# Sparse attention: the compressed branch and the maxima as two streams of their own, with a new order in the scan, the last branch and the combinations

## Chip, core and metric

One Trainium2 chip, one of its cores. The metric is the time of one execution on the device in microseconds (us), as the median of several runs; lower is better. Engines are named as in the profile: PE (TensorE, matrix products; PEld is its weight load), DVE (VectorE), ACT (ScalarE), POOL (GpSimd), SP (SyncE, which issues nearly all DMAs).

## What is computed

A decoder block on 1024 positions of 1024 channels, all in float32. One input projection feeds three mixers; their outputs are projected, weighted with sigmoid gates, summed and projected once more; a gated MLP with a short convolution follows. What the change touches is this:

```python
# sparse attention, 2 key groups of 4 heads, per query t:
o_cmp = softmax(q @ kc + bias) @ vc              # over 63 compressed keys
idx   = top_8(block sums of that softmax)        # which 64-key blocks are selected
o_sel = softmax(q @ k_sel, keys of idx) @ v_sel
o_win = softmax(q @ k_win, last 512 keys) @ v_win
y_nsa = gate[0] * o_cmp + gate[1] * o_sel + gate[2] * o_win
# Mamba-2 scan, in chunks of 128: y = (C B^T * decay * dt) x + C state; then gating and a norm
mixed = g0 * (y_ssm @ w_br_ssm) + g1 * (y_sb @ w_br_sb) + g2 * (y_nsa @ w_br_nsa)
x = x + rms_norm(mixed @ w_out)
u = causal_conv(rms_norm(x) @ w_up)              # then gelu(gate) * val, @ w_down, norm, add
```

## The kernel before

Every float32 product of large matrices is made of three passes over rounded parts (hi times hi, hi times lo, lo times hi); a 128x1024 weight tile is loaded, ACT rounds it to `whi`, POOL subtracts to `wlo` (`load_w`, L290 to 300). All matrix instructions have source line L226, so they are told apart by the names of their tiles. A planner orders the instructions of each engine by its own timing model when the program is built; `tc.keep_in_program_order` pins PE to the order of the text while `in_order[0]` is set (in sparse attention and in the scan), and `tc.issue_after(x)` puts what a block emits on x's engine behind x in that engine's queue.

**Sparse attention** (`nsa_stage`) works on 16 query blocks: 2 groups `g` by 8 blocks of 128 queries `i`. For each, `compressed(g, i)` (L880 to 961) is a generator of nine steps: transposes and the 63 compressed scores, a softmax on DVE and ACT (L902 to L909), for i >= 4 the choice of key blocks down to `aug` (L917 to L930), three steps of nothing, transposes of the probabilities (`pT`, L937), one step later their product with `VC`, then the transposed queries `Q1`, `Q2`. `maxima(g, i)` (L963 to L1000) makes the row maxima of all scores, a product and a DVE reduction (L985) at a time: 8 of them for i < 4 and 16 above, then after `MM_LAG` = 3 steps four transposes and a copy into `Q1` (L1000). `attend()` is a generator that is sent one key block at a time: score, exp, rounding, and four slots later the product with the values; at the end of a branch `merge` and, at the end of a query block, `finish`. All these small pieces share single PSUM banks: `ps_b` has one buffer, `ps_o` one, `ps_s` and `ps_t` two.

The loop over n (L1083 to 1115) runs query block n in slots, the compressed branch of block n+2 and the maxima of block n+1 beside it. A slot sends one key block or none, takes one step of the compressed branch, one of the maxima, some fill (a step of fill is three 512-wide products of a gate projection: 176 steps in all), and one more step of the maxima:

```python
slots = max(NSA_SLOTS, len(blocks)) if n < 16 else NSA_LAG + 6
...
idle = next(ga, 0) == 0                 # compressed
if ready: idle = next(gb, 0) == 0 and idle      # maxima
fill.take(NSA_FILL[0] if b is None else NSA_FILL[1] + idle)
next(att)
if ready: next(gb, 0)
```

The number of key blocks is 2, 4, 6, 8, 10, 11, 12, 13 for i = 0 to 7, so there are 192 slots; 32 steps of fill come before the first.

**The scan** (`ssd_stage`) runs four generators `scan(q, ...)` in staggered turns: `front(c)` of chunk c makes decays `dec` (four ACT instructions L1324, an exp L1327), `ce`, `Bc` (L1343, L1344), `xd` (L1345) and their product (L1347); `back(c)` multiplies them on PE into `ps_b` or `ps_o`. Products of the other two branches (`branches`, L1472 on) fill between; at its end stand the first four half units (j = 0 to 3, first half of the positions) of the last branch, y_ssm @ w_br_ssm, two of them in `ps_s` and two in `dense` banks. `tail_stage` loads their gate rows (`ge`, L1586), multiplies (L1593), adds on POOL (L1594), and goes on with the remaining twelve half units in new `dense` banks.

**The MLP** starts with N_FIRST = 4 pairs of channel tiles made plainly (`up_half`, eight calls, each two units of 24 products, with the convolution L333 to L339 and at the end `gated`, L1728). All later pairs use a seven-product scheme; its right-hand sides are 16 sums and differences of the input (`combos`, L572 to L578, on DVE), rounded by ACT (L1859) and DVE (L1860, L1866).

Of the kernel before, what the change touches and what calls it, by code (L numbers as in the profile page):

```python
# [10 lines left out]
F32 = mybir.dt.float32  # L11
R32 = mybir.dt.float32r
# [205 lines left out]
def trunk(ctx: ExitStack, tc: tile.TileContext, A: dict, outT: bass.AP, dbg=None):  # L218
# [488 lines left out]

    part, ys, begun, weights = {}, {}, {}, {}
    ssd = ExitStack()
# [11 lines left out]
def nsa_stage(nc, tc, es, env):  # L721
# [160 lines left out]
    def compressed(g, i):  # L882
# [32 lines left out]
        if i >= 4:  # L915
# [26 lines left out]
        y = wk.tile([128, 4, 64], F32, name="yacc", bufs=4)  # L942
# [4 lines left out]
        Q1 = wk.tile([128, 512], R32, name="Q1", bufs=3)  # L947
        Q2 = wk.tile([128, 512], R32, name="Q2", bufs=3)
        p1 = ps_b()
# [131 lines left out]
    att = attend()  # L1081
    next(att)
    for n in range(-2, 17):  # L1083
        ga = compressed(*order[n + 2]) if 0 <= n + 2 < 16 else iter(())
        gb = maxima(*order[n + 1]) if 0 <= n + 1 < 16 else iter(())
# [7 lines left out]
        lead = min(NSA_LEAD, slots - nb)  # L1093
        cnt = slots - lead
        blocks = [None] * lead + [next(it) if (m + 1) * nb // cnt > m * nb // cnt else None for m in range(cnt)]
        if n == 7:
            next_keys(1, 0, 384)
            blocks += [None] * NSA_SWITCH[1]
        for m, b in enumerate(blocks):
            att.send(b)  # L1100
# [5 lines left out]
            idle = next(ga, 0) == 0  # L1106
            ready = n != 7 or m >= NSA_SWITCH[0]
            if ready:
                idle = next(gb, 0) == 0 and idle
            fill.take(NSA_FILL[0] if b is None else NSA_FILL[1] + idle)  # L1110
            next(att)
            if ready:
# [181 lines left out]
def ssd_stage(nc, tc, es, env):  # L1294
# [15 lines left out]
    def scan(q, x0, x1, B, C):  # L1310
# [7 lines left out]
        def front(c):  # L1318
# [22 lines left out]
            if c == 0:  # L1341
                states.append(wk.tile([128, 4, 64], F32, name="state"))
            V.tensor_tensor(Bc[:, 1], pt[:, 384:512], E.tri_i, op=OP.mult)  # L1343
# [128 lines left out]
    def branches(ys):  # L1472
        pairs = [(br, j0) for br in (2, 1) for j0 in range(0, 8, 2)]
        parts = [(0, 0), (1, 0), (0, 1), (1, 1)] + [(n, h) for n in range(2, 8) for h in range(2)]
        order = [(pairs[n][0], pairs[n][1] + m, h) for n, h in parts for m in range(2)]
        es = []

# [10 lines left out]
        for n, h in parts:  # L1488
# [15 lines left out]
            if n == 3:  # L1504
                ys[1, h] = sb_rows(h)
        gens = []
        for j in range(2):
            w = ws[8] if j == 0 else E.load_w(A["wb_ssm"][j], 1024)
            out = []
            gens.append(E.half_unit(Bank(), w, lambda k, h: E.ys[k, h], 8, 0, out))  # L1510
            yield from itertools.islice(gens[j], 6)
            E.begun[j, 0] = out[0]
        for g in gens:
            yield from g
        for j in range(2, 4):
            w = E.load_w(A["wb_ssm"][j], 1024)
            out = []
            yield from E.half_unit(E.psd, w, lambda k, h: E.ys[k, h], 8, 0, out)
            E.begun[j, 0] = out[0]
            E.weights[j] = w  # L1520

    held = E.ssm
# [12 lines left out]
    while n == 0 or any(gens):  # L1535
        if n in SSD_ROWS:
            with tc.issue_after(loaded[-1].ins):
                for q, ns, h in SSD_ROWS[n]:
                    E.ssm_rows(q, ns, E.third_t if q % 2 and ns[0] < 4 else E.row_t, h)
        for q, at in enumerate(SSD_AT):  # L1540
            if n == at:
                if q > 1:
                    acs[q] = ac_t(q)
                gens[q] = scan(q, *[held[q][m] for m in range(4)])
            if gens[q]:
                for m in range(1 + (n > at)):
                    if next(gens[q], 0) == 0:
# [14 lines left out]
def tail_stage(nc, tc, es, env):  # L1562
# [21 lines left out]
    for j, h in order:  # L1584
        e = bt.tile([128, 512], F32, name="ge")
        nc.sync.dma_start(e, E.g_d[j * 128:(j + 1) * 128, hs(h)])  # L1586
# [6 lines left out]
        V.tensor_tensor(e, ps, e, op=OP.mult)  # L1593
        P.tensor_tensor(e, E.part[h, j], e, op=OP.add)  # L1594
# [121 lines left out]
    halos = psn.tile([128, 512], F32, name="psn", tag="psn")  # L1716
    even = {}

# [363 lines left out]
```

## Time and profile before

| what | value |
|---|---|
| runs | 2216.98, 2216.97, 2218.39 us; median 2216.98 us |
| profiled execution | 2219.73 us, of which 2218.0 us lie between its first and last instruction |
| busy in the span | PE 2146.9 us (97%), DVE 1351.7 (61%), ACT 1216.8 (55%), POOL 1250.5 (56%) |
| chain that ended last | PE 83%, DVE 6%, ACT 3%, issue 3%, DMA 2%, POOL 2% |
| granted clock, mean | 0.991 |

A busy PE is not a PE at its peak: the ends of its instructions are modelled, so the rate is read from the number of products in a stretch. The waits view lists, for each engine, the time it sat idle and the instruction that ended that. [...]

### The profile page before, as it was taken

To read this page: it belongs to the slowest core of one execution; us is meant where nothing else is said; L and a number is where in the kernel's file an instruction comes from. 1 tells how busy PE (TensorE), PEld (TensorE's weight loads), DVE (VectorE), ACT (ScalarE), POOL (GpSimd) and SP (SyncE) were. 2 spreads that over 40 slices of the span, in tenths; PEclk is the share of its full clock that TensorE was granted. 3 is DMA by queue.
4 is the path that set the end of the run, shared out by engine and by line. 5 is a ranking of instruction groups with operands and counts; after the bars stand their busy time and mean duration, and the time that the engine had idled before them with its cause. 6 is when DMAs were issued, how large, how long until landed. Compare 5 with 4: busy or idle time off the path is not lost.

```text
span 2218.0 us, 30484 instructions
## 1 busy us (share of the span) xinstructions
PE 2146.9 (97%) x10693; PEld 1722.8 (78%) x10693; DVE 1351.7 (61%) x2489; ACT 1216.8 (55%) x2298; POOL 1250.5 (56%) x1099
## 2 busy tenths in 40 slices
PE   7999999999999999999989999999999999999997
PEld 7888889876666678888877777887688888878887
DVE  6765555247647516566546875328865767676786
ACT  6544442456757745677764553236554444476534
POOL 3776642146746743343325685548677777766733
PEclk9999999999999999999999999999999999999999
DMA  4233242421121011212344522335222323255433
GB/s 176 83 110 114 98 133 60 121 86 39 37 88 41 6 55 39 77 67 81 125 162 171 171 83 81 112 113 192 88 84 81 119 95 111 99 178 192 147 107 112
DMA packets 126602, 229.36 MB, mean 103 GB/s; under 512 B 29904, under 2 KB 44016, under 8 KB 126448
## 3 DMA queue, kind: packets, MB, share of 16 engines
q1 hardware_dynamic: 123568, 224.82, 30.3%
q10 hardware_dynamic: 2880, 2.59, 0.3%
q8 instruction: 84, 1.38, 0.2%
q14 instruction: 70, 0.57, 0.1%
HBM read 165.92 MB, written 61.44 MB: 103 GB/s over the span
## 4 chain that ended last, share of the span: by engine, by line
PE 83%; DVE 6%; ACT 3%; issue 3%; DMA 2%; POOL 2%; SPq 0%; DVEq 0%; ACTq 0%; POOLq 0%
PE dense L226 53%; PE ps_s L226 10%; PE ps_t L226 7%; PE ps_o L226 6%; PE ps_b L226 4%; PE psn L226 3%; DMA wraw<-in_wfm 0%; DVE x L1675 0%; ACT wT L1013 0%; POOL wlo L300 0%; POOL h_lo L480 0%; DVE u L337 0%; DVE x L1663 0%; POOL wlo L546 0%; DMA y<-y_d 0%
## 5 line engine op out<-in xcount | busy, mean ns | idle before, releaser
L300 POOL TENSOR_TENSOR wlo<-wraw,whi 128x256 fp32r<-128x256 f32 x304 | 240.5, 823 | 254.6 <-ACT whi L295 248.7
L226 PE MATMUL dense<-h_hi,whi 128*128 128x512 f32 x656 | 262.9, 401 | 2.1 <-DVE row L1153 2.1
L226 PE MATMUL dense<-h_hi,wlo 128*128 128x512 f32 x656 | 256.8, 392 | 1.2 <-POOL wlo L546 1.2
L226 PE MATMUL dense<-h_lo,whi 128*128 128x512 f32 x656 | 256.6, 391 | 0.0
L1024 POOL TENSOR_TENSOR wT_lo<-wT,wT_hi 128x512 fp32r<-128x512 f32 x132 | 168.7, 1288 | 83.3 <-ACT wT_hi L1023 75.2
L226 PE MATMUL dense<-x,uhi 128*128 128x512 f32 x600 | 190.8, 390 | 1.2 <-ACT x L618 1.2
L226 PE MATMUL dense<-hi,whi 128*128 128x512 f32 x448 | 176.2, 394 | 5.0 <-ACT whi L295 5.0
L226 PE MATMUL dense<-hi,wlo 128*128 128x512 f32 x448 | 177.7, 398 | 0.1
L226 PE MATMUL dense<-lo,whi 128*128 128x512 f32 x448 | 176.2, 394 | 1.1 <-POOL lo L1682 1.1
L555 POOL TENSOR_TENSOR ulo<-uf,uhi 128x1024 fp32r<-128x1024 f32 x37 | 88.9, 2403 | 114.2 <-ACT uhi L554 114.2
L226 PEld LDWEIGHTS dense<-h_hi,wlo 128*128 128x128 f32 x656 | 123.1, 188 | 27.9 <-POOL wlo L546 1.6
L226 PEld LDWEIGHTS dense<-h_hi,whi 128*128 128x128 f32 x656 | 123.6, 188 | 25.8 <-DVE row L1153 2.6
L226 PEld LDWEIGHTS dense<-h_lo,whi 128*128 128x128 f32 x656 | 123.5, 188 | 22.7
L226 PEld LDWEIGHTS dense<-x,uhi 128*128 128x128 f32 x600 | 112.4, 188 | 26.0 <-ACT x L618 2.4
L295 ACT ACTIVATE whi<-wraw 128x1024 fp32r<-128x1024 f32 x76 | 80.3, 1057 | 93.1 <-PE dense L226 78.1
L1227 POOL TENSOR_TENSOR s_lo<-sa,s_hi 128x512 fp32r<-128x512 f32 (+2 forms) x48 | 53.9, 1123 | 132.6 <-ACT s_hi L1226 127.2
L985 DVE TENSOR_REDUCE mx<-ps_t 128x1 f32<-128x384 f32 (+3 forms) x192 | 98.7, 520 | 48.3 <-PE ps_t L226 44.9
L337 DVE SCALAR_TENSOR_TENSOR u<-dense,pv,u 128x510 f32<-128x510 f32 (+1 forms) x140 | 103.4, 741 | 39.3 <-ACT u L333 39.3
L558 POOL TENSOR_TENSOR ulo<-uf,uhi 128x1024 fp32r<-128x1024 f32 x37 | 88.9, 2404 | 43.8 <-ACT uhi L557 41.9
L1013 ACT ACTIVATE wT<-ps_s 128x512 f32<-128x512 f32 x132 | 78.3, 595 | 57.1 <-PE ps_s L226 52.9
L226 PEld LDWEIGHTS dense<-hi,whi 128*128 128x128 f32 x448 | 85.0, 190 | 25.2 <-ACT whi L295 6.3
L226 PE MATMUL dense<-x,ulo 128*128 128x512 f32 x264 | 102.9, 390 | 0.0
(560 smaller groups left out, 6231.3 us busy)
## 6 DMA issues: line engine op xcount, KB each, us to landing
wraw<-in_wfm SPq DMA_DIRECT2D x62, 512.0 KB, 3.9
wraw<-in_wup SPq DMA_DIRECT2D x48, 512.0 KB, 3.7
lo<-m_d SPq DMA_DIRECT2D x58, 256.0 KB, 3.3
g_d<-gate_e SPq DMA_DIRECT2D x48, 256.0 KB, 2.0
s_d<-o SPq DMA_DIRECT2D x48, 256.0 KB, 2.1
m_d<-u SPq DMA_DIRECT2D x44, 256.0 KB, 2.0
row<-s_d SPq DMA_DIRECT2D x32, 256.0 KB, 4.5
row<-g_d SPq DMA_DIRECT2D x32, 256.0 KB, 3.9
```

The costliest lines, as they stand in the source:

```text
L226: i = f(*a, **k)
L295: act(hi, raw, AF.Copy)
L300: (V if tiles else P).tensor_tensor(lo[:, s], raw[:, s], fl(hi[:, s]), op=OP.subtract)
L337: V.scalar_tensor_tensor(o[:, d:], ps[:, :512 - d], taps[d], o[:, d:], op0=OP.mult, op1=OP.add)
L555: P.tensor_tensor(l24, f24, fl(h24), op=OP.subtract)
L558: P.tensor_tensor(l31, f31, fl(h31), op=OP.subtract)
L985: V.tensor_reduce(mx[:, h, a, n:n + 1], pm[:, :w], axis=AX, op=OP.max)
L1013: act(w.rearrange("p h q -> p (h q)"), pz, AF.Exp)
L1024: P.tensor_tensor(lo, wf, fl(hi), op=OP.subtract)
L1227: (P if SB_SLO else V).tensor_tensor(s_lo[:, c0:], a[:, c0:], fl(s_hi[:, c0:]), op=OP.subtract)
```

## The change

In sparse attention both generators become a `Stream` that goes on to the next block by itself. The compressed branch may run up to three blocks ahead of the block that attends, the maxima up to two; the maxima of a block start when its compressed branch ended at least one slot ago. `compressed` gets two more empty steps (one behind the softmax, one behind `pT`), so eleven steps. The slots of a block are at least ten (nine for n = 8, 9), one more than its key blocks where those are 10 or 11, 13 for the two turns ahead of block 0, and two extra at n = 7. No fill is taken ahead of the stage. `yacc` has 5 buffers for 4, `Q1` and `Q2` have 4 for 3.

In the scan the tile `state` is placed ahead of `xd` and `Bc`, and what the first scan's second `front` issues on ACT and DVE is queued behind the exp and the product of its first. The gating of the last branch's first four half units moves from the tail to where each ends in `branches`, with gate rows loaded there by the same look-ahead; the second unit gets 4 steps ahead instead of 6. The combinations on DVE are queued behind the fifth `gated` of the MLP.

```diff
-NSA_SLOTS = 9
+NSA_SLOTS = 10
+NSA_START = 13
-NSA_EARLY = 32
-NSA_LEAD = 0
-NSA_SWITCH = (10, 1)
+NSA_EARLY = 0
+NSA_AHEAD = 3, 2
+NSA_SWITCH = (10, 2)
...
-        for _ in range(3):
+        for _ in range(4):
             yield
...
         act(pT.rearrange("p a b -> p (a b)"), pt[:, :256], AF.Copy)
         yield
+        yield
...
+    sa = Stream(compressed, lambda k, n, m: k <= n + NSA_AHEAD[0])
+    sb = Stream(maxima, lambda k, n, m: (k + 1 < sa.done or k < sa.done and slot[0] > sa.at + 1)
+                and k <= n + NSA_AHEAD[1]
+                and (k < 8 or n > 7 or n == 7 and m >= NSA_SWITCH[0]))
...
-        slots = max(NSA_SLOTS, len(blocks)) if n < 16 else NSA_LAG + 6
+        slots = NSA_START if n < 0 else NSA_LAG + 6 if n == 16 else max(NSA_SLOTS - (n in (8, 9)), nb + (nb in (10, 11)))
...
+            work = sa.step(n, m)
+            work = sb.step(n, m) or work
+            fill.take(NSA_FILL[0] if b is None else NSA_FILL[1] + (not work))
             next(att)
-            if ready:
-                next(gb, 0)
-        for _ in itertools.chain(ga, gb):
-            pass
+            sb.step(n, m)
+        while n < 15 and (sa.done < min(n + 3, 16) or sb.done < n + 2):
+            ...
# scan
+            if c == 0:
+                states.append(wk.tile([128, 4, 64], F32, name="state"))
             xd = wk.tile([128, 2, 4, 64], F32, name="xd", bufs=4)
...
+                    with ExitStack() as behind:
+                        if n == 1 and (q, m) == (0, 0):
+                            behind.enter_context(tc.issue_after(act_marks[0].ins))
+                            behind.enter_context(tc.issue_after(dve_marks[0].ins))
+                        ended = next(gens[q], 0) == 0
# last branch
+        order += [(0, j, 0) for j in range(4)]
...
+        def evict(j):
+            gate_rows()
+            e = es.pop(0)[0]
+            V.tensor_tensor(e, outs[j][0], e, op=OP.mult)
+            P.tensor_tensor(E.part[0, j], E.part[0, j], e, op=OP.add)
+            E.begun.add(j)
...
-            yield from itertools.islice(gens[j], 6)
+            yield from itertools.islice(gens[j], k)       # k = 6, 4
-        for g in gens:
+        for j, g in enumerate(gens):
             yield from g
+            evict(j)
...
-        if (j, h) in E.begun:
-            ps = E.begun[j, h]
+        if h == 0 and j in E.begun:
+            e = E.part[h, j]
# MLP
-        V.tensor_tensor(m, st["gelu", h], st[1, h], op=OP.mult)
+        gate_marks.append(V.tensor_tensor(m, st["gelu", h], st[1, h], op=OP.mult))
...
-        E.combos(*lows, V)
+        with tc.issue_after(gate_marks[N_FIRST].ins):
+            E.combos(*lows, V)
```

## Rows read from the trace of the kernel before

**Rows 1.** The page: busy us, share of the span and count of instructions of each engine; and of its costliest groups that of the weights' `wlo` pieces on POOL (line, engine, operation, tiles, shapes, count | busy us, mean ns | idle before, and what ended it).

```profile
PE 2146.9 (97%) x10693; PEld 1722.8 (78%) x10693; DVE 1351.7 (61%) x2489; ACT 1216.8 (55%) x2298; POOL 1250.5 (56%) x1099
...
L300 POOL TENSOR_TENSOR wlo<-wraw,whi 128x256 fp32r<-128x256 f32 x304 | 240.5, 823 | 254.6 <-ACT whi L295 248.7
```

**Rows 2.** Busy time by stretch: sparse attention, the start of the MLP, and an undisturbed piece of the MLP. Columns: stretch, its length, busy time and instructions of each engine, granted clock, DMA share, GB/s.

```profile
440.00:757.00 317.00, 300.72 (x1673) 210.01 (x1672) 200.55 (x520) 215.86 (x488) 190.17 (x233) 0.99 0.18 54
...
1560.00:1631.00 71.00, 65.37 (x268) 51.93 (x267) 59.15 (x86) 36.76 (x54) 49.39 (x46) 0.95 0.26 85
1700.00:1900.00 200.00, 200.00 (x884) 165.68 (x883) 132.80 (x228) 97.03 (x135) 145.24 (x85) 1.00 0.30 104
```

**Rows 3.** Busy time by stretch, as in Rows 2: first the stretch behind one wait of sparse attention, then the five stretches between 440 and 2200 us in which half the clock was granted.

```profile
602.80:606.20 3.40, 1.94 (x14) 1.52 (x13) 1.50 (x6) 2.22 (x7) 3.01 (x3) 1.00 0.01 2
691.00:694.40 3.40, 3.34 (x10) 2.39 (x11) 2.21 (x8) 0.70 (x2) 2.98 (x5) 0.50 0.00 0
1162.00:1168.90 6.90, 6.15 (x21) 4.20 (x22) 4.46 (x10) 1.87 (x5) 0.00 (x0) 0.51 1.03 376
1366.80:1373.70 6.90, 6.27 (x15) 4.92 (x16) 4.67 (x6) 1.05 (x2) 1.65 (x1) 0.51 0.43 148
1595.50:1598.90 3.40, 3.40 (x10) 2.62 (x9) 3.40 (x5) 0.38 (x1) 3.40 (x4) 0.50 0.08 14
1609.20:1612.60 3.40, 3.40 (x9) 2.48 (x8) 3.40 (x7) 2.81 (x4) 3.40 (x5) 0.50 0.00 0
```

**Rows 4.** PE's waits in sparse attention (440 to 757 us). Columns: the tile PE was to write, what ended the wait; us in total, times, longest.

```profile
PE ps_s L226 <- DVE Q L1000: 3.3, 4, 0.9
PE ps_b L226 <- ACT pT L937: 2.8, 4, 0.8
PE ps_b L226 <- DVE cp L909: 2.6, 2, 1.5
PE ps_t L226 <- DVE MM L995: 2.1, 3, 1.0
PE ps_o L226 <- ACT oT L1037: 1.3, 4, 0.6
PE ps_b L226 <- DVE of L1048: 1.3, 1, 1.3
PE ps_b L226 <- DVE aug L930: 1.1, 1, 1.1
PE ps_b L226 <- DVE MM L995: 1.0, 1, 1.0
```

**Rows 5.** PE's waits from 1150 to 1372 us, columns as in Rows 4.

```profile
PE ps_b L226 <- DVE dec L1347: 3.7, 1, 3.7
PE dense L226 <- DVE ge L1593: 3.2, 1, 3.2
...
PE dense L226 <- POOL wlo L300: 1.1, 1, 1.1
```

**Rows 6.** The timeline at the scan's start. Columns: start and length in us, engine, line, operation, out<-in, count, and in brackets the idle time before it and what ended it.

```profile
1154.09 1.12 ACT L1324 ACTIVATE dec<-dense,acu 128x128 f32<-128x128 f32 x4
...
1158.76 1.20 ACT L1327 ACTIVATE dec<-dec 128x512 f32<-128x512 f32 x2
...
1161.32 0.69 DVE L1345 TENSOR_TENSOR xd<-ps_t,dte 128x512 f32<-128x512 f32 x1 [0.98 <-DMA g_d<-gate_e]
...
1162.75 0.66 PE L226 MATMUL ps_b<-dec,xd 128*64 128x128 f32 x3 [3.75 <-DVE dec L1347]
```

**Rows 7.** The timeline at the start of the tail, columns as in Rows 6.

```profile
1361.06 0.69 DVE L1593 TENSOR_TENSOR ge<-ps_s,ge 128x512 f32<-128x512 f32 x1 [3.57 <-DMA ge<-g_d]
...
1361.83 1.29 POOL L1594 TENSOR_TENSOR ge<-lo,ge 128x512 f32<-128x512 f32 x1 [5.50 <-DVE ge L1593]
...
1364.30 1.40 DVE L1399 SCALAR_TENSOR_TENSOR row<-third,pv,ps_t 128x512 f32<-128x512 f32 x2
...
1366.70 0.68 DVE L1593 TENSOR_TENSOR ge<-dense,ge 128x512 f32<-128x512 f32 x1
...
1367.43 1.22 PE L226 MATMUL dense<-row,whi 128*128 128x512 f32 x2 [3.23 <-DVE ge L1593]
```

**Rows 8.** PE's waits for ACT from 1560 to 1631 us, columns as in Rows 4.

```profile
PE dense L226 <- ACT whi L295: 4.4, 2, 2.5
```

**Rows 9.** Groups of DVE's instructions from 1577 to 1612 us. Columns: line, operation, tiles, shapes, count | busy us, mean ns | idle before.

```profile
L337 DVE SCALAR_TENSOR_TENSOR u<-dense,pv,u 128x511 f32<-128x511 f32 (+1 forms) x9 | 6.5, 737 | 0.0
L1860 DVE TENSOR_TENSOR x<-x 128x512 fp32r<-128x512 f32 x7 | 6.4, 929 | 0.0
```

**Rows 10.** The timeline from 1585 to 1596 us, columns as in Rows 6.

```profile
1587.41 2.84 POOL L1792 TENSOR_TENSOR ulo<-uf,uhi 128x1024 fp32r<-128x1024 f32 x1
...
1587.92 2.88 DVE L577 TENSOR_TENSOR x<-x 128x512 f32<-128x512 f32 x1
...
1590.84 1.15 ACT L1859 ACTIVATE x<-x 128x512 fp32r<-128x512 f32 x2 [5.38 <-DVE x L577]
...
1593.14 0.68 DVE L577 TENSOR_TENSOR x<-x 128x512 f32<-128x512 f32 x1
...
1593.65 0.50 PE L226 MATMUL dense<-hi,whi 128*128 128x512 f32 x1 [2.50 <-ACT whi L295]
...
1594.89 1.23 DVE L576 TENSOR_TENSOR x<-x 128x512 f32<-128x512 f32 x1
```

More of the change, by code (lines that the diff above doesn't have):

```diff
@@ L706, in lo_t @@
         return lop.tile([128, 512], dt, name="lo", bufs=16)
-    part, ys, begun, weights = {}, {}, {}, {}
+    part, ys, begun, weights = {}, {}, set(), {}
     ssd = ExitStack()
@@ L941, in compressed @@
             mm(po[:, a * 128:(a + 1) * 128], pT[:, a, :], VC[g], start=True, stop=True)
-        y = wk.tile([128, 4, 64], F32, name="yacc", bufs=4)
+        y = wk.tile([128, 4, 64], F32, name="yacc", bufs=5)
         V.tensor_tensor(y, po.rearrange("p (h d) -> p h d", h=4),
@@ L945, in compressed @@
         yield
-        Q1 = wk.tile([128, 512], R32, name="Q1", bufs=3)
-        Q2 = wk.tile([128, 512], R32, name="Q2", bufs=3)
+        Q1 = wk.tile([128, 512], R32, name="Q1", bufs=4)
+        Q2 = wk.tile([128, 512], R32, name="Q2", bufs=4)
         p1 = ps_b()
@@ L1082, in nsa_stage, with __init__, step @@
     next(att)
+    slot = [0]
+    class Stream:
+        def __init__(self, make, ok):
+            self.make, self.ok, self.g, self.done, self.at = make, ok, None, 0, 0
+        def step(self, n, m=0):
+            if self.g is None:
+                if self.done > 15 or not self.ok(self.done, n, m):
+                    return False
+                self.g = self.make(*order[self.done])
+            if next(self.g, 0) == 0:
+                self.g = None
+                self.done += 1
+                self.at = slot[0]
+            return True
+    sa = Stream(compressed, lambda k, n, m: k <= n + NSA_AHEAD[0])
+    sb = Stream(maxima, lambda k, n, m: (k + 1 < sa.done or k < sa.done and slot[0] > sa.at + 1)
+                and k <= n + NSA_AHEAD[1]
+                and (k < 8 or n > 7 or n == 7 and m >= NSA_SWITCH[0]))
     for n in range(-2, 17):
-        ga = compressed(*order[n + 2]) if 0 <= n + 2 < 16 else iter(())
-        gb = maxima(*order[n + 1]) if 0 <= n + 1 < 16 else iter(())
         blocks = []
@@ L1089, in nsa_stage @@
             blocks = [(g, i, a, kb) for a in range(2) for kb in range(max(0, i - 4) if a else 0, i + 1)]
-        slots = max(NSA_SLOTS, len(blocks)) if n < 16 else NSA_LAG + 6
         nb = len(blocks)
+        slots = NSA_START if n < 0 else NSA_LAG + 6 if n == 16 else max(NSA_SLOTS - (n in (8, 9)), nb + (nb in (10, 11)))
         it = iter(blocks)
-        lead = min(NSA_LEAD, slots - nb)
-        cnt = slots - lead
-        blocks = [None] * lead + [next(it) if (m + 1) * nb // cnt > m * nb // cnt else None for m in range(cnt)]
+        blocks = [next(it) if (m + 1) * nb // slots > m * nb // slots else None for m in range(slots)]
         if n == 7:
@@ L1099, in nsa_stage @@
         for m, b in enumerate(blocks):
+            slot[0] += 1
             att.send(b)
@@ L1105, in nsa_stage @@
                 next_keys(1, 384, T)
-            idle = next(ga, 0) == 0
-            ready = n != 7 or m >= NSA_SWITCH[0]
-            if ready:
-                idle = next(gb, 0) == 0 and idle
-            fill.take(NSA_FILL[0] if b is None else NSA_FILL[1] + idle)
-            next(att)
-            if ready:
-                next(gb, 0)
-        for _ in itertools.chain(ga, gb):
-            pass
+            work = sa.step(n, m)
+            work = sb.step(n, m) or work
+            fill.take(NSA_FILL[0] if b is None else NSA_FILL[1] + (not work))
+            next(att)
+            sb.step(n, m)
+        while n < 15 and (sa.done < min(n + 3, 16) or sb.done < n + 2):
+            if sa.done < min(n + 3, 16):
+                sa.step(n, 99)
+                slot[0] += 2
+            if sb.done < n + 2:
+                sb.step(n, 99)
     df = E.dta.rearrange("p c h -> p (c h)")
@@ L1546, in ssd_stage @@
                 for m in range(1 + (n > at)):
-                    if next(gens[q], 0) == 0:
+                    with ExitStack() as behind:
[3 more added lines that the diff above has]
+                        ended = next(gens[q], 0) == 0
+                    if ended:
                         gens[q] = None
@@ L1584, in tail_stage @@
     for j, h in order:
-        e = bt.tile([128, 512], F32, name="ge")
-        nc.sync.dma_start(e, E.g_d[j * 128:(j + 1) * 128, hs(h)])
-        if (j, h) in E.begun:
-            ps = E.begun[j, h]
-        else:
+        if h == 0 and j in E.begun:
+            e = E.part[h, j]
+        else:
+            e = bt.tile([128, 512], F32, name="ge")
+            nc.sync.dma_start(e, E.g_d[j * 128:(j + 1) * 128, hs(h)])
             if j not in E.weights:
@@ L1592, in tail_stage @@
             ps, = fm_unit(psd, E.weights[j], lambda k, h: E.ys[k, h], 8, halves=(h,))
-        V.tensor_tensor(e, ps, e, op=OP.mult)
-        P.tensor_tensor(e, E.part[h, j], e, op=OP.add)
+            V.tensor_tensor(e, ps, e, op=OP.mult)
+            P.tensor_tensor(e, E.part[h, j], e, op=OP.add)
         hi, lo = mix[h, j] = hi_t(), lo_t()
@@ L1716, in tail_stage @@
     halos = psn.tile([128, 512], F32, name="psn", tag="psn")
-    even = {}
+    even, gate_marks = {}, []
     def in_pairs(f):
```

15 lines of the change are left out of this document (5 added, 10 removed).

## The prediction

> **What bounds the kernel now.** I read the page first: PE is busy 97% of the span [rows 1]. That share alone says nothing of its rate, so next the stretches: where nothing disturbs it, PE runs 884 products in 200 us [rows 2], 0.226 us for one of 512 columns. The products stay the same in number and size under this change; it can only win or lose time in which PE waits, and time in which PE runs at half the clock. The waits view tells where PE waits. Sparse attention has 317.0 us with 300.7 of them busy, so 16.3 us idle [rows 2]; the scan's start and the tail's start lose 3.7 and 3.2 us at one point each [rows 5]; the start of the MLP loses 4.4 us at two [rows 8]. [...]
>
> I make the sum against the profiled execution, 2219.7 us; the median of the runs is 2217.0, 2.7 us lower, and I give the forecast on that footing. About 0.2%, 4.4 us, can be told from no change.
>
> **Part A, the two streams.** What they remove is the fixed tie of the two generators to the block. Of the 16.3 us, five kinds of wait stand at `ps_b`, the bank of the compressed branch: for `pT` 2.8, for `cp` 2.6, for `of` 1.3, for `aug` 1.1, for `MM` 1.0, together 8.8 us in nine waits, none over 1.5 us [rows 4]. In each, PE comes to a step before DVE or ACT finished the step ahead of it (`of` and `MM` only tell what DVE had in its queue instead). A slot lasts 317.0 / 192 = 1.65 us. The new empty step behind the softmax gives the `cp` transposes one more slot, which is more than the longest wait; `aug` comes later by two; the second new step gives `pT` one. So all 8.8 us should go. The other waits of that view stay: `Q` 3.3, `MM` at `ps_t` 2.1, `oT` 1.3. For `Q` I counted turns: block 4 leaves the compressed branch at turn 55, its maxima take ten turns from turn 57, and its first score follows turn 66 (13 + 13 + 4 x 10). They end in the last slot before they are needed, as they do now; the same holds for block 5 and in the second group.
>
> Fill is conserved. Each of 176 steps costs 3 x 0.226 us wherever it stands. Slots rise from 192 to 211, those without a key block from 60 to 79; two steps in each make 120 + 32 taken ahead now, and 158 later, the rest in idle turns, with two steps left over. So no slot runs dry, and giving up the 32 early steps costs nothing: the 26 slots ahead of block 0 hold 52. The four loads of a compressed block (`q_in`, twice `qd`, the bias) go up to one block earlier past the gate stores on SP; the DMA engines are 18% busy there [rows 2], so I cost that at nothing; were they late, a block's first step would wait.
>
> What is late next? DVE still has its 520 instructions in the stretch [rows 2], now in other places. The bounds are that no wait returns, and that all 8.8 us return. I take three waits of the mean size, 3.0 us, since the new place has an empty slot more. With the half clock after 691 us gone (1.7), part A gives 8.8 - 3.0 + 1.7 = **7.5 us**; bounds 0 and 10.5.
>
> **Part B, the scan's start.** PE waited 3.75 us for the product with `dec` [rows 6]. ACT had the four pieces of the first `front` by 1155.2 but made its exp only at 1158.8, behind work of the second `front`; then DVE, in order, stood before the second `xd` until 1161.3, which the profile puts down to a gate store that still read that memory. Queued ahead, the exp (0.60 us) can end at 1155.8 and `xd` and the product (0.69 and about 0.64) at 1157.2 even if both follow it, while PE arrives at 1162.75 - 3.75 = 1159.0: covered by 1.8 us. If `state`, placed first, moved the first `xd` onto that store, the product would again wait for 1161.3 and the gain would be near 0; the first `xd` ran without such a wait, so I take it as free. 3.7 us and the clock's 3.4 us go; next come the roundings of the loaded rows on DVE, for which I allow one such operation, 0.7 us. Part B gives 3.7 + 3.4 - 0.7 = **6.4 us**; bounds 0 and 7.1.
>
> **Part C, the last branch.** At the tail's start DVE waited 3.57 us for the first gate row, and PE 3.23 us until the fourth product [rows 7]: the new units take banks that those products free. With rows loaded ahead and the products made where the units end, only the last one remains: 0.7 us plus a start of about 0.2, so 0.9; with the norm's two operations (1.40 us) ahead of it on DVE, 2.3. I take 0.9. The clock's 3.4 us go. The four gate loads move ahead of weight loads on SP, and two POOL adds (1.29 us each [rows 7]) ahead of the next unit's `wlo` pieces, where PE already waits 1.1 us [rows 5]. Against that, the second unit now has two more steps (6 x 0.226 = 1.4 us) behind the first as cover. Bounds for that place: 1.1 gained, and 2 x 1.29 - 1.4 = 1.2 lost; I take 0, between them. What a gate load that holds SP would cost nothing shows; the weights behind it would be late at the same place. Part C gives 3.2 - 0.9 + 3.4 = **5.7 us**; bounds 0 and 7.7.
>
> **Part D, the combinations.** Here a queue is blocked: ACT sat idle 5.38 us before a rounding (L1859) that waited for a combination on DVE [rows 10], and the next weights' `whi` stood behind it; PE waited 2.5 us at 1593.65 and 1.9 us once more [rows 8]. With the 16 combinations behind the fifth `gated`, the first of these goes, with its half clock (1.7). The second can come back, since ACT's roundings still follow combinations that DVE delays; I leave its 1.9 and 1.7 us.
>
> New is a deadline. The fifth `gated` can come about 2.5 us (two convolution steps of 0.74 [rows 9], ACT's part and its own 0.68, as an operation of that size takes [rows 10]) after its unit ends at 1593.65 - 2.50 = 1591.2, so at 1593.6. Three calls of 48 products follow (32.6 us), then two products of the first seven-product pair that need no combination (5.4 us): the third needs them from 1629.2, the last of its four about 2 us later. In these 37.6 us DVE must do 16 combinations, 8 roundings, and the convolutions and gatings of about five units, 5 x (2 x 0.74 + 0.5) + 3 x 0.68 = 12 us [rows 9], with an allowance of 0.5 for their edges. So 24 operations may take 25.6 us, 1.07 us each. One takes 0.68 us with POOL quiet, 1.23 beside POOL's 256-wide pieces, and 2.88 beside a 1024-wide one of 2.84 [rows 10]. POOL is busy 49.4 of 71.0 us there [rows 2], with 256-wide pieces: 0.68 + 0.70 x 0.55 = 1.06 us. It just fits (today's roundings, 0.93 in the mean [rows 9], say the same); I allow 1.0 us. At 1.23 each PE would be 3.9 us late, at 0.68 not at all. Part D gives 2.5 + 1.7 - 1.0 = **3.2 us**; bounds 0.3 and 7.8.
>
> [...]
>
> **Sum.** 7.5 + 6.4 + 5.7 + 3.2 = 22.8 us. 2219.7 - 22.8 = 2196.9 for a profiled execution; 2217.0 - 22.8 = **2194** for the median.
>
> **The rivals.**
> 1. *Sparse attention keeps its waits elsewhere.* DVE's queue, not the number of empty steps, sets them: it is busy 63% of that stretch, and two of the five kinds name DVE work of other generators [rows 2, 4]. Against it: no wait exceeds a slot. Part A is then worth 0: 2194 + 7.5 = 2202.
> 2. *The waits go, the slow clock stays.* An idle 1.5 us behind 602.8 was followed by full clock [rows 3], the 1.3 us for `of` [rows 4], which ended at 691.0, by half; so a small wait that remains can be enough. All of A's, B's, C's and D's clock terms, 10.2 us, fail: 2204.
> 3. *Slower: the combinations miss the first pair.* Place: PE at the third product of the first pair. If all 24 operations take the 2.88 us seen beside a wide POOL operation, DVE needs 69 + 12 us where it has 37.6: 43 us of waiting, 2237. It begins at 1.07 us each and turns the sign at 1.07 + 22.8 / 24 = 2.0 us. Against it: the wide operations of the early weights are over by 1590.3 [rows 10]. [...]
> 4. *The change does not do what it says.* The planner moves work so that DVE and the banks still come in the old order: A, B and C give nothing, 2214.
>
> **How the numbers follow.** Forecast 0.58, rival 1 0.16, rival 2 0.12, rival 3 0.05, rival 4 0.09. Faster: 0.58 + 0.16 + 0.12 = 0.86; same 0.09; slower 0.05. All upper bounds together would give 33.1 us, 2184, and some of the waits left out of A (6.7 us) may shift too: the low end is 2181. Rivals 1 and 2 together give 2212; the high end is 2211. Rivals 3 and 4 stay outside, 0.14.
>
> **What would show it.** Right: no waits for `pT`, `cp` or `aug` at `ps_b`, those for `Q` still four of about 0.9 us; no idle PE ahead of the first `dec` product; under 1 us at the first `dense` unit of the tail; no ACT idle over 2 us between 1580 and 1595; full clock at three or more of the five places. Wrong: a stretch of sparse attention over 312 us for the same products, a wait for the combinations' roundings at the first seven-product pair, or a large new wait at a place not named here.

## The result, and the profile after

The changed kernel takes 2199.80 us (median of 5 runs, 2198.39 to 2201.04) against 2216.98: 0.9921 of the time, 95% interval 0.9907 to 0.9934. That is 17.2 us faster where 22.8 were forecast, 2199.8 where 2194 stood, inside the range. The profiled execution took 2201.04 us, its span 2199.3. PE's row on the page, against [rows 1]: the products are the same.

```profile
PE 2142.9 (97%) x10693; PEld 1717.6 (78%) x10693; DVE 1347.5 (61%) x2489; ACT 1214.7 (55%) x2298; POOL 1251.6 (57%) x1099
```

**Where it was gained.** Since the products are the same in number and size, the start of the same product in both traces tells what came about ahead of it. After against before: first product with `rtab` (behind sparse attention) 3.4 us earlier, first with `sel` (scan) 2.6, last with `dec` 4.3, first with `osq` (behind the last branch) 10.9, last with `osq` 11.1, first with `ulo` behind that (seven-product pairs) 19.9, first with `fhi` 18.4, end 18.7. Between any two of these there are equally many products in every kernel here. So in this pair of executions A gave 3.4, B 0.8 (counted from `rtab` to the last `dec`), C 6.6 and D 8.8, where 7.5, 6.4, 5.7 and 3.2 were forecast: the sum is near, the terms are not.

**Sparse attention.** PE's waits of the changed kernel from 300 to 839.6 us, columns as in [rows 4]:

```profile
PE ps_t L227 <- DVE mx L987: 2.5, 6, 0.8
PE ps_s L227 <- ACT wT L1015: 2.4, 5, 0.7
PE ps_b L227 <- ACT qT L893: 2.0, 3, 1.3
PE ps_o L227 <- ACT oT L1039: 1.7, 3, 0.6
PE ps_b L227 <- DVE Q L962: 0.8, 2, 0.4
PE ps_s L227 <- DVE kd L833: 0.8, 1, 0.8
...
PE ps_o L227 <- POOL wT_lo L1026: 0.7, 1, 0.7
PE ps_b L227 <- DVE yacc L945: 0.6, 1, 0.6
...
PE ps_b L227 <- DVE Q L956: 0.6, 1, 0.6
PE ps_o L227 <- ACT wT_hi L1025: 0.4, 1, 0.4
PE ps_s L227 <- DVE K L840: 0.3, 1, 0.3
```

All kinds of [rows 4] but `oT` are gone, `Q` at `ps_s` and `MM` at `ps_t` with them; `mx`, `wT`, `qT`, `kd` and `K` are new or larger. One more wait of the kernel before, behind the stretch of [rows 4], left as well:

```profile
PE dense L226 <- DVE row L1153: 2.1, 1, 2.1
```

Busy time from 300 us, where both kernels are at the same product to within one, to the first product with `rtab`, before and after:

```profile
300.00:842.98 542.98, 522.87 (x2901) 397.57 (x2900) 273.63 (x704) 314.11 (x679) 263.34 (x323) 1.00 0.21 63
```

```profile
300.00:839.53 539.53, 524.81 (x2901) 395.97 (x2901) 274.09 (x704) 311.91 (x680) 262.77 (x323) 1.00 0.21 63
```

Idle fell from 20.1 to 14.7 us, but PE is busy 1.9 us longer with the same 2901 products. One new wait has a plain cause, at the start of the stage (timeline, columns as in [rows 6]):

```profile
402.74 0.36 ACT L270 ACTIVATE sg<-dtr 128x192 f32<-128x192 f32 x1 [0.60 <-DVE dtr L762]
...
404.00 0.29 ACT L867 ACTIVATE da<-da 128x128 f32<-128x128 f32 x1
404.19 0.36 ACT L893 ACTIVATE qT<-ps_b 128x256 f32<-128x256 f32 x1
...
404.61 0.71 PE L227 MATMUL ps_b<-KC,qT 128*128 128x128 f32 x4 [1.27 <-ACT qT L893]
```

ACT does six short operations (402.74 to 404.29) before it copies `qT`. The 32 fill steps that stood ahead of the stage had covered them. The same holds for `kd` and `K`, at which PE waits ahead of the stage: these three waits, 2.4 us, are in every kernel here without the 32 steps and in none with them.

**The scan's start**, against [rows 6]:

```profile
1154.07 0.62 ACT L1349 ACTIVATE dec<-dec 128x512 f32<-128x512 f32 x1
...
1156.42 0.69 DVE L1523 TENSOR_TENSOR lo<-ps_s,row 128x512 f32<-128x512 f32 x1 [2.90 <-PE ps_s L227]
...
1157.03 0.68 DVE L1367 TENSOR_TENSOR xd<-ps_t,dte 128x512 f32<-128x512 f32 x1
1157.63 0.68 DVE L1369 TENSOR_TENSOR dec<-dec,Bc 128x512 f32<-128x512 f32 x1
...
1158.46 1.05 PE L227 MATMUL ps_b<-dec,xd 128*64 128x128 f32 x8 [2.07 <-DVE dec L1369]
```

The exp is ready at 1154.7, ahead of PE as forecast. But DVE, in order, stands before a row product of the last branch (L1523) until PE ends a unit at 1156.3, and only then makes `xd` and the product. The wait shrank from 3.75 to 2.07 us. The kernel before has the same row product ahead of its `xd`:

```profile
1159.04 0.69 DVE L1500 TENSOR_TENSOR lo<-ps_s,row 128x512 f32<-128x512 f32 x1 [1.10 <-PE ps_s L226]
```

**The last branch**, against [rows 7]: the fourth product is gone from PE's path, one of 0.69 us is left.

```profile
1358.72 0.69 DVE L1532 TENSOR_TENSOR row<-dense,row 128x512 f32<-128x512 f32 x1 [1.60 <-PE dense L227]
...
1359.46 0.74 PE L227 MATMUL dense<-row,whi 128*128 128x512 f32 x2 [0.35 <-DVE row L1532]
```

**The start of the MLP.** Neither wait of [rows 8] is there. Groups of DVE's instructions from 1580 to 1622 us, as in [rows 9]:

```profile
L1894 DVE TENSOR_TENSOR x<-x 128x512 fp32r<-128x512 f32 x8 | 7.4, 963 | 0.0
...
L577 DVE TENSOR_TENSOR x<-x 128x512 f32<-128x512 f32 x4 | 4.1, 1086 | 0.0
L578 DVE TENSOR_TENSOR x<-x 128x512 f32<-128x512 f32 x4 | 3.6, 948 | 0.0
L579 DVE TENSOR_TENSOR x<-x 128x512 f32<-128x512 f32 x4 | 3.6, 920 | 0.0
...
L576 DVE TENSOR_TENSOR x<-x 128x512 f32<-128x512 f32 x4 | 2.7, 737 | 0.0
```

The 16 combinations and 8 roundings take 0.94 us each (mean of the five rows by count). They begin at 1583.98 and end at 1608.64, ahead of the first pair, whose first `ulo` product is at 1618.4. In this time DVE and POOL ran side by side, for instance here (timeline):

```profile
1586.63 4.12 DVE L577 TENSOR_TENSOR x<-x 128x512 f32<-128x512 f32 x4
...
1586.93 4.41 POOL L301 TENSOR_TENSOR wlo<-wraw,whi 128x256 fp32r<-128x256 f32 x4 [2.58 <-ACT whi L296]
```

**The clock**, against [rows 3]: stretches by window. The first two are all at half the clock between 50 and 2189 us; the other two are the places of 1366.8 and 1595.5.

```profile
1158.60:1162.00 3.40, 3.40 (x14) 2.60 (x13) 1.99 (x5) 2.35 (x5) 0.00 (x0) 0.50 1.06 397
1261.00:1264.40 3.40, 3.40 (x21) 2.32 (x20) 3.40 (x3) 1.38 (x4) 3.40 (x4) 0.50 0.22 65
1355.50:1362.40 6.90, 6.55 (x31) 5.19 (x30) 3.78 (x6) 2.42 (x4) 2.60 (x2) 1.00 0.25 96
1579.50:1582.90 3.40, 3.40 (x17) 2.82 (x16) 2.79 (x7) 2.22 (x3) 3.40 (x5) 1.00 0.12 35
```

Products of 512 columns in the stretch at 1595.5 of the kernel before (timeline):

```profile
1595.89 0.63 PE L226 MATMUL dense<-lo,whi 128*128 128x512 f32 x1
1596.32 0.63 PE L226 MATMUL dense<-hi,wlo 128*128 128x512 f32 x1
1596.75 0.63 PE L226 MATMUL dense<-hi,whi 128*128 128x512 f32 x1
...
1598.45 0.62 PE L226 MATMUL dense<-lo,whi 128*128 128x512 f32 x1
```

They start every 0.427 us (1595.89 to 1598.45, six steps), where [rows 2] have one in 0.226 at full clock. So 3.4 us at 0.50 cost 1.6 us there. Counting half the length, 1.7, is an estimate and 0.1 us above that; the sums below keep it.

1261.0 is not among the stretches of [rows 3]. Ahead of it stands a wait of 1.2 us (`ps_t`, the norm's L263) which the kernel before has as well, with full clock behind it.

### The profile page after: what moved, and what is told of

Its sections match the earlier page's. It is cut to its first block, busy times and chain, and to the rows that moved or that the text cites. A ratio compares the mean times of both kernels' runs of the same rounds, so it can differ in the third digit from the quotient of the medians.

```text
span 2199.3 us, 30490 instructions
## 1 busy us (share of the span) xinstructions
PE 2142.9 (97%) x10693; PEld 1717.6 (78%) x10693; DVE 1347.5 (61%) x2489; ACT 1214.7 (55%) x2298; POOL 1251.6 (57%) x1099
## 4 chain that ended last, share of the span: by engine, by line
PE 80%; DVE 6%; ACT 4%; issue 3%; POOL 3%; DMA 2%; SPq 0%; DVEq 0%; ACTq 0%; POOLq 0%
PE dense L227 51%; PE ps_s L227 10%; PE ps_t L227 6%; PE ps_o L227 6%; PE ps_b L227 3%; PE psn L227 3%; ACT wT L1015 1%; POOL wlo L301 0%; DMA wraw<-in_wfm 0%; DVE mx L987 0%; POOL h_lo L481 0%; POOL wlo L547 0%; DVE u L338 0%; DMA augf<-in_c_aug 0%; ACT wT_hi L1025 0%
## 5 line engine op out<-in xcount | busy, mean ns | idle before, releaser
L1015 ACT ACTIVATE wT<-ps_s 128x512 f32<-128x512 f32 x132 | 78.4, 596 | 52.8 <-PE ps_s L227 49.0
L547 POOL TENSOR_TENSOR wlo<-wraw,whi 128x1024 fp32r<-128x1024 f32 x37 | 90.4, 2443 | 20.8 <-ACT whi L546 20.5
```

The costliest lines, as they stand in the source:

```text
L547: P.tensor_tensor(wlo, raws[0], fl(whi), op=OP.subtract)
L1015: act(w.rearrange("p h q -> p (h q)"), pz, AF.Exp)
```

## The experiments

**Each part alone on the kernel before** (on one chip). Each edit is the part's own hunks of the diff above; their core, from A to D:

```diff
+    sa = Stream(compressed, lambda k, n, m: k <= n + NSA_AHEAD[0])
...
+                            behind.enter_context(tc.issue_after(act_marks[0].ins))
+                            behind.enter_context(tc.issue_after(dve_marks[0].ins))
...
+            yield from g
+            evict(j)
...
+        with tc.issue_after(gate_marks[N_FIRST].ins):
+            E.combos(*lows, V)
```

> The kernel before with part A alone (two streams, new steps, deeper buffers). If the parts simply add, as the starts of the same products in the two traces say (A 3.4 us, B 0.8, C 6.6, D 8.8), this is 3.4 us faster than before, about 2213.6: the nine waits at ps_b go, waits for mx, wT and qT of some 6 us take their place, and the half clock at 691 us is full. By the forecast's term it is 7.5 us faster, 2209.5. By rival 1 (waits only elsewhere) it is within 1 us of before.

> The kernel before with part B alone (state ahead of xd, the second front behind the first). If the parts add: 0.8 us faster, 2216.2, and in the profile PE still waits 1.5 to 2.5 us at the first product with dec, since DVE reaches the first xd only behind a row product that waits for PE's last product ahead of dec. By the forecast's term: 6.4 us faster, 2210.6, and no wait there. If the half clock behind it falls from 6.8 to 3.4 us and no new stretch comes elsewhere, 3 to 4 us faster.

> The kernel before with part C alone (gate rows loaded ahead, products made where the units end). If the parts add: 6.6 us faster, 2210.4, with a wait below 0.6 us at the first dense unit of the tail and full clock behind it. By the forecast's term 5.7 us, 2211.3: these two differ by less than they can be told apart by time, so the profile's wait for wlo decides (0.4 against 1.1 us). If the gain hangs on A or B ahead of it, under 4 us.

> The kernel before with part D alone (the combinations behind the fifth gated). If the parts add: 7.5 to 8.8 us faster, 2208 to 2209.5, both waits for whi at the start of the MLP gone, with both half clock stretches. By the forecast's term: 3.2 us faster, 2213.8, the second wait (1.9 us) and its half clock left. If the second wait went only because the other parts moved the weights' loads, it is still there and the gain is 4 to 5 us.

| alone | us, median | ratio to before, 95% | in the profile |
|---|---|---|---|
| A | 2210.73 | 0.9973 (0.9960 to 0.9985) | first `rtab` product 3.7 us earlier |
| B | 2214.75 | 0.9989 (0.9980 to 0.9999) | wait at `dec` 2.1 us, behind the row product |
| C | 2212.98 | 0.9983 (0.9974 to 0.9992) | tail's waits 0.3 (`row`) and 0.2 us (`wlo`) |
| D | 2210.40 | 0.9970 (0.9958 to 0.9981) | both waits for `whi` gone |

The gains add to 0.85%, 18.8 us against 17.2 for all four; with intervals of 2 to 3 us to either side of each, the parts add as far as can be told. D's second wait went without the others' help, so that sub-theory falls. A's 6.0 us, B's 2.4 and D's 6.7 lie between the forecast's terms and those of the pair of traces, and their intervals reach far (A's from 3.3 to 8.9). C's gain of 3.8 us (1.8 to 5.8) stays below the 6.6 of the pair. The waits there hardly differ between the profiles (`ge` 2.4 to 3.2 us and `wlo` 1.1 without C, 0.3 and 0.2 with it), so that points to the clock; see the repeats below.

In A alone PE's wait at the first `dec` product is 2.7 us, for 3.3 to 3.7 in the other kernels without B: there the second `xd` runs without the wait for the gate store. So beside A, B takes out 0.6 us of that wait and no more.

**What holds DVE at the scan's start.**

```diff
-                    if n == 0:
-                        fill.take(SSD_AHEAD)
-                    if n >= SSD_FROM and (q > 1 or n < at + 9):
-                        fill.take(SSD_FILL[m])
+                    with tc.issue_after(dve_marks[0].ins) if n < 2 else nullcontext():
+                        if n == 0:
+                            fill.take(SSD_AHEAD)
+                        if n >= SSD_FROM and (q > 1 or n < at + 9):
+                            fill.take(SSD_FILL[m])
```

> The changed kernel, with the row products of the fill in the scan's first two rounds queued on DVE behind the first product with dec. If a row product that waits for PE is what kept DVE from the first xd (after: row product at 1156.42, xd 1157.03, dec product 1157.63, PE waits 2.07 us), the order is now xd, dec product, row product; the product can end by 1154.7 (exp ends at 1154.7 plus 0.7 at most 1155.4), PE's wait of 2.07 us goes, and with it perhaps the half clock behind (1.7): 2.1 to 3.8 us faster than the changed kernel, 2196.0 to 2197.7. If the bank that a row product frees is what PE needs next, the wait moves to ps_s ahead of dec: no gain. If ACT's exp decides, a wait of 1 to 2 us stays at dec.

2197.18 us (2196.63 to 2200.11). DVE at the scan's start:

```profile
1153.00 0.69 DVE L1367 TENSOR_TENSOR xd<-ps_t,dte 128x512 f32<-128x512 f32 x1 [2.62 <-ACT Bc L1366]
1153.61 0.68 DVE L1369 TENSOR_TENSOR dec<-dec,Bc 128x512 f32<-128x512 f32 x1
1154.21 0.68 DVE L1523 TENSOR_TENSOR lo<-ps_s,row 128x512 f32<-128x512 f32 x1
```

PE has no wait at the first `dec` product, which starts at 1156.52, and full clock behind it. The row product was the blocker. What that is worth in time this run does not show: against the kernel before on its own chip the ratio is 0.9920, where the changed kernel's was 0.9921.

**How far the combinations' deadline is.**

```diff
-        with tc.issue_after(gate_marks[N_FIRST].ins):
+        with tc.issue_after(gate_marks[N_FIRST + 2].ins):
```

> The changed kernel, with the 16 combinations behind the seventh gated instead of the fifth, two units or 21.8 us later. In the changed kernel they and their 8 roundings took 24.7 us (1583.98 to 1608.64), 0.90 us each with the convolutions between; the first pair's third product came near 1618.4 + 5.4 = 1623.8, so 15 us were to spare. Two units later they end near 1630: PE late by 5 to 9 us at the first pair, 2205 to 2209. By the forecast's 1.06 us each, 24 x 1.06 + 2.5 = 28 us from 1605.6: 10 us late. If the queue order alone matters and the deadline is far, no loss: within 2 us of the changed kernel.

2207.55 us (2206.38 to 2208.97), 7.8 above the changed kernel. PE's waits from 1560 to 1660 us, and three of DVE's rows:

```profile
PE dense L227 <- ACT snap L1730: 2.4, 2, 2.2
PE psn L227 <- DVE x L1900: 1.8, 1, 1.8
PE dense L227 <- DVE x L1894: 1.4, 2, 0.9
...
PE dense L227 <- ACT x L1893: 0.5, 1, 0.5
```

```profile
1604.79 2.48 DVE L576 TENSOR_TENSOR x<-x 128x512 f32<-128x512 f32 x4
1607.20 6.89 DVE L577 TENSOR_TENSOR x<-x 128x512 f32<-128x512 f32 x4
...
1627.19 2.27 DVE L1894 TENSOR_TENSOR x<-x 128x512 fp32r<-128x512 f32 x1
```

The time is within the 2205 to 2209 us expected, and the deadline of the forecast is real: here the 24 operations need from 1604.8 to 1634.0, and PE waits at the first pair. In the change it lies some 15 us away, by the sum in the expectation.

**Part A taken apart.** First the two steps and buffers without the streams, then the streams without the steps.

```diff
-        for _ in range(3):
+        for _ in range(4):
             yield
...
         act(pT.rearrange("p a b -> p (a b)"), pt[:, :256], AF.Copy)
         yield
+        yield
...
-        y = wk.tile([128, 4, 64], F32, name="yacc", bufs=4)
+        y = wk.tile([128, 4, 64], F32, name="yacc", bufs=5)
```

(`Q1` and `Q2` from 3 to 4 buffers likewise.) The second kernel is A alone less the two added `yield` steps.

> The kernel before with only the two empty steps of the compressed branch and the deeper buffers; one block's two generators stay tied to the slots of a block. If the empty steps alone cure the waits, pT, cp and aug go at ps_b and the first product with rtab comes 3 us or more earlier than before (842.98). If the steps need the two streams, a block now has more steps than its slots, the rest runs on at the block's end without cover, and that product comes later than before, by a few us.

> Part A without the two empty steps: the streams, slots and buffers, on the kernel before. If the empty steps are what takes the waits for pT, cp and aug out, these are back here, 4 to 6 us of them, and the first product with rtab stands near that of before (842 to 844). If the streams' spreading does it, they stay out, and it stands near 839.3 as in part A alone.

Both are slower than before: 2233.78 us, ratio 1.0088 (1.0072 to 1.0103), and 2224.81 us, 1.0041 (1.0027 to 1.0055). PE's waits from 395 to 900 us, steps alone and then streams alone:

```profile
PE ps_b L226 <- DVE Q L955: 15.8, 11, 2.5
PE ps_s L226 <- DVE Q L1001: 4.7, 4, 1.5
PE ps_b L226 <- DVE Q L961: 3.7, 8, 0.8
```

```profile
PE dense L227 <- DVE row L1174: 3.3, 1, 3.3
PE ps_b L227 <- DVE cp L910: 3.0, 3, 1.4
PE ps_o L227 <- ACT oT L1038: 2.3, 5, 0.6
```

The steps do take out `pT`, `cp` and `aug`; but a tied block then has more steps than slots, 24 us of waits for `Q` follow, and the first `rtab` product is at 860.6, 17.6 us later than before, with 20.5 us of half clock ahead of it. The streams alone bring `cp` back, but only 0.7 us of `pT`, so the expected 4 to 6 us are not all there; the first `rtab` product is at 851.4, later than either theory said, with 10.2 us of half clock ahead of it. Alone, each half costs time; together they gain it.

**Repeats, and the rest of B.** The changed kernel and the one with the row products behind again, unchanged and side by side; the kernel before again; and B's queue order alone, which is B less this edit. The last two ran once each.

```diff
+            if c == 0:
+                states.append(wk.tile([128, 4, 64], F32, name="state"))
             xd = wk.tile([128, 2, 4, 64], F32, name="xd", bufs=4)
```

> The changed kernel again, as the yardstick of rows_behind_2 on the same chip, and for a second profile. If the stretches at half the clock belong to the kernel, its profile shows those at 1158.6 and 1261.0 us again; if they follow waits by chance, one of them is missing or another place has one (1139 us, behind 2.4 us of waits that the first profile also had). Its time against before: 0.990 to 0.994.

> The changed kernel with the row products queued on DVE behind the first product with dec, a second time, beside the changed kernel. If the 2.07 us wait that it takes out is the gain, it is 2 to 4 us faster than the changed kernel here too; if the lower times of its first run were the chip's, the two are within 1 us.

> The kernel before, for a second profile. If the half clock stretches belong to the kernel, they are at 691, 1162, 1367, 1595 and 1609 us again. If they follow waits by chance, 1162 (6.8 us, in every profile so far of a kernel with that wait of 3.7 us) comes back, and 691 and 1367, which the other kernels with the same work there did not show, stay out; waits in us are the same.

> The kernel before with only the queue order of part B: the second front behind the first, state left behind xd and Bc. If the placing of state moved xd away from the memory of a gate store, the first or second xd waits here for that store again, as at 1161.3 in the kernel before, and the product with dec comes later than in part B alone (1160.4). If the queue order does it all, that product is at 1160.4 again, with the wait of about 1.9 us behind the row product.

Changed: 2199.51 us, 0.9929 (0.9916 to 0.9943). With the row products behind: 2198.46, 0.9919 (0.9906 to 0.9933). The medians are 1.1 us apart, the means 2.0, between the two expectations, and the intervals overlap; over both sets the means are 2200.2 (10 runs) and 2198.1 (9), 2.1 us apart, while in the profiles the first `dec` product is 2.0 us and the last 3.8 us earlier in the mean. Likely faster, not proven at this size. B's queue order alone: 9.69 us from the first `sel` product to the first `dec` product, as in B alone (9.70); the placing of `state` did nothing.

The kernel before took 2223.28 us in its one run. Its waits are those of the first profile to 0.1 us in sparse attention, but its clock is in part another:

```profile
528.30:535.10 6.80, 6.28 (x23) 4.79 (x24) 2.84 (x8) 2.62 (x5) 2.17 (x2) 0.50 0.07 20
695.50:698.90 3.40, 3.40 (x14) 2.39 (x12) 2.25 (x9) 0.92 (x2) 2.53 (x5) 0.51 0.00 0
1166.60:1173.40 6.80, 5.96 (x20) 4.02 (x21) 4.55 (x10) 1.78 (x5) 0.00 (x0) 0.50 1.05 393
1371.40:1374.80 3.40, 3.27 (x8) 2.59 (x9) 3.40 (x5) 0.63 (x1) 1.65 (x1) 0.50 0.43 154
```

From 690 us on this execution is 4 to 5 us later than the first, so that 695.5, 1166.6, 1371.4 and 1613.7 lie, to within 1 us, at the places of 691, 1162, 1367 and 1609 in the first: four of five came back, one of them half as long, where 691 and 1367 were expected to stay out; 1595 is missing, and 528 and 607 are new.

Starts and lengths (us) of the stretches at 0.50 in twelve profiles (the two halves of A are left out), without the kernel's first 50 us and its end:

| profile | stretches |
|---|---|
| before | 691.0 (3.4), 1162.0 (6.8), 1366.8 (6.8), 1595.5 (3.4), 1609.2 (3.4) |
| before, again | 528.3 (6.8), 606.8 (3.4), 695.5 (3.4), 1166.6 (6.8), 1371.4 (3.4), 1613.7 (3.4) |
| A alone | 1584.7 (3.4) |
| B alone | 1160.8 (3.4), 1587.4 (3.4) |
| B's queue order | 691.6, 1142.1, 1162.6, 1589.3 (3.4 each) |
| C alone | 1161.7 (6.8), 1588.4 (3.4), 1602.0 (3.4) |
| D alone | 1161.7 (6.8), 1264.1 (3.4) |
| changed | 1158.6 (3.4), 1261.0 (3.4) |
| changed, again | 1259.6 (3.4) |
| rows behind, twice | 1139.1 (3.4); 1139.0 (3.4) |
| combinations late | 1139.8, 1160.3, 1624.5 (3.4 each) |

With these twelve profiles each part can be told over several executions, by the time between the same products (mean, range, number of profiles). B's row leaves out the two with the row products behind, D's the one with the combinations late:

| part | between | without | with | gain |
|---|---|---|---|---|
| A | start, first `rtab` | 843.4 (842.2 to 847.0), 6 | 839.2 (838.9 to 839.5), 6 | 4.2 |
| A | first `rtab`, first `sel` | 309.0 (308.4 to 309.8), 6 | 309.8 (309.2 to 310.1), 6 | -0.8 |
| B | first `sel`, last `dec` | 196.0 (193.0 to 197.4), 5 | 194.1 (193.6 to 195.1), 5 | 1.9 |
| C | last `dec`, first `osq` | 136.0 (134.6 to 138.3), 6 | 131.7, 6 | 4.3 |
| D | last `osq`, first `ulo` | 77.5 (76.8 to 78.4), 6 | 69.4, 5 | 8.1 |
| D | first `ulo`, first `fhi` | 330.3, 6 | 332.1, 5 | -1.8 |

Sum 15.9 us; the runs give 2217.0 (mean of 41 of the kernel before) less 2200.2 (10 of the changed) = 16.8. The mean granted clock rose from 0.9925 to 0.9956, 0.0031 x 2217 = 6.9 us if PE is busy all the time. So up to 7 us are clock, and about 10 are waits, net: PE's idle time fell by 14.7 us in the mean of the two profiles of either kernel (71.1 and 72.4 to 56.4 and 57.7), but PE at full clock is busy some 4 us longer (2134.9 and 2135.5 to 2139.5 and 2138.4, with half the length of the stretches above taken off).

## Why the prediction was right, and where its steps failed

The direction and the mechanism held: queues and a bank's turn kept PE waiting, and the change moved that work. The total was 5.6 us too high, and that it came as near is in part luck: by the twelve profiles A, B and C fell short of their terms by 10.0 us together, and D was 3.1 above its own. The terms for the clock (1.7 us in A and in D, 3.4 in B and in C) are half the length of a stretch at 0.50, a price that no run shows: products started every 0.427 us there against 0.226, which is 1.6 us of 3.4, and the stretches came and went from one execution to the next.

- **Part A, 7.5 forecast, 3.4 measured (4.2 less 0.8).** The nine waits at `ps_b` went, as said. "Three waits of the mean size, 3.0 us" failed: `mx`, the growth of `wT` and `oT`, `qT`, `kd` and `K`, `Q` at `ps_b` and three smaller ones make 10.7 us. "The other waits of that view stay" failed to the good side: `Q` at `ps_s` and `MM`, 5.4 us, left too, and so did a wait of 2.1 us for `row` (L1153) behind the stretch, which had no term. Counting turns gave the wrong answer there, since the deeper `Q` buffers and the stream let the maxima run earlier than they must. "Giving up the 32 early steps costs nothing" failed by 2.4 us of these, 1.3 for `qT` and 1.1 for `kd` and `K`: the fill was conserved, its cover of ACT and DVE was not. Idle time fell by 5.4 us, close to the net 5.8 of the sum, and the clock's 1.7 us came out in the mean: three of six profiles without A have slow stretches there, 20.4 us together, none with A has. But PE is busy longer for the same products, which no step had: from 300 us to `rtab` 524.2 to 524.8 us in A alone and both profiles of the changed kernel, 521.1 to 521.9 in B, C and D alone, none of them with a slow stretch there. So these 3 us belong to part A; why stays open.
- **Part B, 6.4 forecast, 1.9 measured.** The failed step is "can end at 1157.2". It asked when ACT's exp and DVE's two operations could run, not what else stood ahead of them on DVE: the row product, whose wait for PE shows in the before trace too, and which the sum did not count. The wait fell by 1.7 us, not 3.7, and part A alone takes 0.6 to 1.0 of that. With that product moved behind, the wait is 0. The clock's 3.4 us failed too: between these products there are 6.1 us of half clock in the mean of the profiles without B and 4.1 with it, 1.0 us of gain. That `state` might move `xd` onto a store's memory was rightly taken as free.
- **Part C, 5.7 forecast, 4.3 measured.** The mechanism was right. The wait left is 0.35 us (0.9 forecast), and the `wlo` wait fell from 1.1 to 0.2 at that place, 0.9 of the 1.1 at the upper bound. The 3.4 us of clock failed: of six profiles without C only two have a stretch there, 6.8 and 3.4 us, in the mean 0.9 us of loss.
- **Part D, 3.2 forecast, 6.3 measured (8.1 less 1.8).** "The second can come back" failed: with the combinations in one block, ACT's roundings and `whi` alternate, and both waits went, 4.4 us instead of 2.5, with the clock behind both. The deadline was met with 15 us of room, so the 1.0 us allowed for it was not lost: an operation took 0.94 us where 1.06 was expected, and with POOL quiet they start every 0.60 us though each takes 0.68; and of the 12 us allowed for convolutions and gatings only 3.9 fell between the 24. Of the 1.8 us lost behind, some 1.0 is waits at `snap` and `wlo` around the first pairs; the rest is not settled. The sign "no ACT idle over 2 us" failed harmlessly: ACT idles 4.40 us before 1591.92, but PE has no wait for the `whi` behind it.
- **DVE beside POOL.** Of the 24 operations none took longer than 1.23 us in the changed kernel, beside 256-wide POOL pieces. Where both engines had work, the starts on either were 1.15 us apart; a piece then took some 1.18 us, and 0.74 elsewhere. With the combinations late, four of them (L577) took 6.89 us together, 1.72 each, beside 512-wide POOL operations that started every 1.70 us, and one rounding took 2.27 us beside a 1024-wide one of 2.41. In the changed kernel POOL was idle for 1.81 to 2.58 us ahead of each four pieces, and 11 of the 24 took 0.68 us or less: hence the mean of 0.94 us, and nothing like the 2.88 us that rival 3 supposes for all.
- **Rivals.** Rival 1 was half right: A's waits came back elsewhere, and more of the old ones left. Rival 2 was half right: a clock stretch stayed at 1158.6 and another came. (The wait that ended at 691.0 was one of 1.13 us for `cp`; the 1.3 for `of` ended at 581.0, with full clock behind it.) Rival 3's price was seen only with the combinations two units later, and then 7.8 us, since the late ones still took 1.08 us each. Rival 4 fell with A, B and C alone, by little with B. Rivals 1 and 2 together give 2210, not 2212: part A's 1.7 us of clock is in both.
- **The signs.** No wait for `pT`, `cp` or `aug`, 0.35 us at the tail's first unit, and full clock at four of the five places came as said; the four waits for `Q` at `ps_s` went, and PE is idle ahead of the first `dec` product. Whether sparse attention stayed under 312 us cannot be told: fill that stood ahead of it is now inside.

## What to carry to other kernels

When a step is to be "queued ahead", list everything that stands ahead of it on its engine in order, and what each of those waits for: a product of another stream that waits for PE can take the place of the wait removed (here one that stood 2.90 us left 2.07 of 3.75). The waits of one trace could be summed as terms here, since they came back in a second profile of the same kernel, to 0.1 us in sparse attention and at the tail with 2.8 us for 3.2; the half-clock stretches could not, since that profile had only four of the five, one half as long, and two others. Two edits that look like one tuning each (more steps, freer streams) can both lose alone and win together: try them together before dropping either.

## What was not expected of the hardware

The same wait was followed by half the clock in one execution and by full clock in another. In the kernel before, a wait of 1.46 us for `cp` ended at 604.5 us with full clock behind it [rows 3], and in its second profile at 607.0 with half the clock from 606.8. Around 1137 us PE waits 1.1 us for `s_hi` and 0.9 us for `w_hi`, in the changed kernel as with the row products behind. The stretch behind these waits, first with the row products behind, then in the changed kernel:

```profile
1139.10:1142.50 3.40, 3.40 (x10) 2.66 (x9) 1.67 (x4) 1.26 (x2) 0.00 (x0) 0.50 0.86 296
```

```profile
1139.60:1143.00 3.40, 3.40 (x16) 2.71 (x15) 1.59 (x4) 1.87 (x3) 0.00 (x0) 1.00 0.97 353
```

10 products against 16 in the same time. In 41 runs of the kernel before the mean clock is 0.991 to 0.994; its two profiles are both at 0.991, so that the forecast counted clock from the low end. What decides whether a wait is followed by half the clock, no run here shows.
